# Turning h by VectorE as it comes about, in place of turning it again in the gate stage

## The chip, the core and the metric

The kernel runs on one core of one Trainium2 chip. Five engines, TensorE (PE), VectorE (DVE), ScalarE (ACT), GpSimd (POOL) and SyncE (SP), each take their own instructions in order and meet at semaphores. The metric is device time in microseconds; less is better. One execution is also profiled.

## The reference

One step of a layer of a streaming encoder over 2048 new frames and 32 frames of a running stream, 1024 channels, float32:

```python
hn = rmsnorm(h, g_mix)
proj = hn @ w_in                       # then two mixers: a short convolution, pooling windows
...
h = h + jnp.concatenate([yA, yB], axis=-1) @ w_out
gate = jax.nn.sigmoid(rmsnorm(h, g_ple) @ w_ple_gate)
h = h + (p @ w_ple) * gate
...
return rmsnorm(h, g_final), ...
```

The case turns on the line with `w_out`, which makes h, and the line with `w_ple_gate`, which needs h with channels on the partitions.

## The kernel before, in words

The work goes through stages in time: the projection w_in with the mixers (to about 545 us), some of the embedding p @ w_ple (to 553), **w_out's stage** (553 to 715), the rest of the embedding (715 to 755), the **gate stage** (755 to 924) and a tail.

Frames come in 17 tiles: sixteen of 128 frames and a short one of 32. In both stages two tiles are taken together as a pair (loop L1327 in w_out's stage; the pair of tiles i and i+1 is called oi there). A pair is multiplied by a 1024x1024 weight with seven products in place of eight (`seven`): the frames' parts are named 11, 12, 22 and the sums S1 to S4 (`frame_parts`, L193; each made by a DVE add or subtract), the weights' parts 11, 21, 22 and the differences T1 to T4. Every part is split in a high and a low half (`split`, L76 to L78: an ACT copy, a DVE subtract), and each product is 12 matmuls of 128x512 into one of three PSUM banks, X, Y and Z. The banks are read between products by DVE: a *carry* keeps a partial result (`c_o`), an *out* adds the final one into x (L1234). Products of X follow each other, so X must have been read before the next of them starts: 11·11, S2·T2, S3·T3, 22·T4 in that order.

In w_out's stage the mixers' result y, already turned, is loaded from memory (y_d) as two tiles of 512 KB for each pair (`load_y`, L314), x is loaded for each tile (`load_rows`, L327), and when both halves of a tile of x hold h, `done_h` (L1260) sums its squares on ACT (into rs_h by GpSimd, L69 and L73) and stores the tile to h_d from SyncE's queue. In the same stage the gate's weight rows are scaled: `gs` loaded by GpSimd (L1284), scaled by ACT, stored to g_d from ACT's queue.

In the gate stage h is loaded again in two ways: as it is, for the final sum, and turned, for the products. The turning differs for the two tiles of a pair:

- `turned` (the even tile and the short one): one load of h_d, two ACT copies that bring the channels in the gate's order (`ho`), eight PE transposes into two PSUM banks (`pth`, L1396).
- `turned_here` (the odd tile): four loads of 32 partitions each in pieces of 1 KB, and a DVE transpose of 32x32 blocks in place (`hn`, L1407). The gate's weight rows are kept in memory in the matching order of channels.

Buffers: pool `ya` (5 of 128x1024: y, first x, the upper rows of w_out, then hn, e and others), `qa` (2 of 128x512: gs, then ho), `xh` (3: x and h), `st`, `ss`, `cmb` for carries, sums and splits. A buffer's next load waits until the last reader of its old content is done. A scheduler orders each engine's instructions from the program; `tc.issue_after` and `tc.keep_in_program_order` hold some of them in place. SyncE issues the loads of y, x and the stores of h one after the other, each waiting for what it needs, so a load that waits holds up all that stand behind it.

Of the kernel before, what the change touches and what calls it, by code (L numbers as in the profile page):

```python
# [15 lines left out]
P = 128  # L16
D = 1024
# [17 lines left out]
def trunk(ctx, tc, x_p, x_s, c_conv, c_pool, p_p, p_s, g_mix, w_in, conv_w, conv_b, pool_w,  # L35
# [9 lines left out]
    e_d = tc.dram_tile([T, D], F32, name="e_d")  # L45
    g_d = tc.dram_tile([D, D], F32, name="g_d")
# [283 lines left out]
    with ExitStack() as s1:  # L330
# [884 lines left out]
    with ExitStack() as s2:  # L1215
        pool = lambda name, bufs: s2.enter_context(tc.tile_pool(name=name, bufs=bufs, reuse_waits="tile"))
        w3, qa, xh, st, ss, cmb = (pool(*a) for a in (
            ("w3", 1), ("qa", 2), ("xh", 3), ("st", 4), ("ss", 3), ("cmb", 8)))
# [43 lines left out]
        def prep_h(i):  # L1262
            lo, hi = load_y(i, 2 * P) if i else first_y
            S[i], more = frame_parts(cmb, ss, f"y{i}", lo[:, :, :P], hi[:, :, :P], lo[:, :, P:], hi[:, :, P:])
            return more

        def short(name, parts, n):
            A = []
            for half, t in enumerate(parts):
                c = cmb.tile([P, KH, 2, P], F32R, tag="c", name=f"{name}_{half}")  # L1270
                c = c.rearrange("p k h n -> p k (h n)")
                split(c[:, :, :n], c[:, :, n:2 * n], t[:, :, :n])
                A.append(c)
            return A

        def scale_gate(k):
# [4 lines left out]
            ts = [qa.tile([P, NH], F32, tag="q", name=f"gs_{k}_{half}") for half in range(2)]  # L1281
# [35 lines left out]
        more = prep_h(0)  # L1317
# [9 lines left out]
        for i in range(0, NT - 1, 2):  # L1327
            with tc.issue_after(loaded[-1].ins):
                x = [load_rows(xh, "x", i + b, x_p) for b in range(2)] if i else [first_x, second_x]
            seven(f"o{i}", S.pop(i), W, *h_ops(x, P, f"o{i}", i == 0), {0: {1: rest}, 2: {3: next_gate}}.get(i, {}), True, i == 0)  # L1330
            for b in range(2):
                done_h(i + b, x[b])
            last = i + 4 == NT - 1
            if last:
                n = tiles[NT - 1][1]
                A = short("yl", load_y(NT - 1, n), n)
# [27 lines left out]
        def ring(what, i):  # L1364
# [4 lines left out]
            return ring4(ya, f"e{what}_{i}")  # L1369
# [16 lines left out]
        def turned(i):  # L1386

            r, n = tiles[i]
            t = load_rows(ya, "hn", i, h_d).rearrange("p (q k c) -> p k q c", q=4, k=KC)
            out = []  # L1390
            for half in range(2):
                pt = tbank(f"pth_{i}_{half}")
                o = qa.tile([P, KH, P], F32, tag="q", name=f"ho_{i}_{half}")
                nc.scalar.copy(o[:n].rearrange("p k (q c) -> p k q c", q=4), t[:n, half * KH:half * KH + KH])
                for k in range(KH):
                    nc.tensor.transpose(pt[:, k * P:k * P + n], o[:n, k], ident[:n, :n])  # L1396
                out.append(pt.rearrange("p (k t) -> p k t", k=KH))
            return out

        def turned_here(i):  # L1400

            r, n = tiles[i]
            t = ring4(ya, f"hn_{i}")
            for q in range(4):
                nc.sync.dma_start(t[q * 32:q * 32 + 32].rearrange("p (g c) -> p g c", g=4),
                                  h_d[r:r + P, q * 256:q * 256 + 256].rearrange("(g p) c -> p g c", p=32))
            nc.vector.transpose(t, t)  # L1407
            u = t.rearrange("p (g k t) -> p k g t", g=4, k=KC)
# [47 lines left out]
        def last_pair(i, A):  # L1456
# [6 lines left out]
            e = load_rows(ya, "e", i, e_d)  # L1463
# [65 lines left out]
        def prep_g(i):  # L1529
# [4 lines left out]
            def put(q, src, view=lambda t: t):  # L1534
                A[q] = cmb.tile([P, KH, 2, P], F32R, tag="c", name=f"g{i}_{q}")
                split(view(A[q][:, :, 0]), view(A[q][:, :, 1]), src)

            def comb(q, x, y, op, view=lambda t: t):
                t = ss.tile([P, KH, P], F32, tag="s", name=f"g{i}_f{q}")
                nc.vector.tensor_tensor(view(t), x, y, op=op)  # L1540
                return t

            lower = []

            def first():
                lower.extend(turned_here(i + 1))

            def second():
                a21, a22 = lower
                s1 = comb("S1", a21, a22, ALU.add, whole)  # L1550
                a11, a12 = turned(i)
                put("11", a11)
                s2 = comb("S2", s1, a11, ALU.subtract)
                s3 = comb("S3", whole(a11), a21, ALU.subtract, whole)
                put("12", a12)
                put("S2", s2)
                s4 = comb("S4", a12, s2, ALU.subtract)
                put("S1", s1)
                put("S3", s3)
                put("S4", s4)  # L1560
                put("22", a22, whole)
# [6 lines left out]
        A = short("gl", turned(NT - 1), n)  # L1568
# [4 lines left out]
        h, e = (load_rows(*a) for a in ((xh, "h", NT - 1, h_d), (ya, "e", NT - 1, e_d)))  # L1573
# [39 lines left out]
```

## Time and profile before

| what | value |
|---|---|
| median of 3 runs | 937.44 us (937.44, 938.89, 936.55) |
| profiled execution | 935.15 us, of which the span of instructions 933.4 us |
| mean granted TensorE clock | 0.998 |
| PE busy | 917.5 us, 98% of the span |
| DVE / ACT / POOL busy | 716.9 / 482.2 / 126.3 us |
| DMA moved | 190.05 MB, 204 GB/s in the mean |

How to read it: busy time is a mean over stages; the chain of waits says what ended last; the timelines give each instruction's start, its length, and in brackets the engine's idle time before it and what ended that. Times of a timeline count from the span's start.

### The profile page before, as it was taken

To read this page: it belongs to the slowest core of one execution; us is meant where nothing else is said; L and a number is where in the kernel's file an instruction comes from. 1 tells how busy PE (TensorE), PEld (TensorE's weight loads), DVE (VectorE), ACT (ScalarE), POOL (GpSimd) and SP (SyncE) were. 2 spreads that over 40 slices of the span, in tenths; PEclk is the share of its full clock that TensorE was granted. 3 is DMA by queue.
4 is the path that set the end of the run, shared out by engine and by line. 5 is a ranking of instruction groups with operands and counts; after the bars stand their busy time and mean duration, and the time that the engine had idled before them with its cause. 6 is when DMAs were issued, how large, how long until landed. Compare 5 with 4: busy or idle time off the path is not lost.

```text
span 933.4 us, 13100 instructions
## 1 busy us (share of the span) xinstructions
PE 917.5 (98%) x4581; PEld 827.8 (89%) x4581; DVE 716.9 (77%) x1215; ACT 482.2 (52%) x895; POOL 126.3 (14%) x244
## 2 busy tenths in 40 slices
PE   8999999899999999999999999999999999999996
PEld 7999999899999999999999987888878868888885
DVE  7997988989577868585777679665564798888985
ACT  7734564644445554443545446344334875555664
POOL 3111132211001110000000011111211001211113
PEclk9999999999999999999999999999999999999999
DMA  9357587597945547328656359766775884566563
GB/s 266 84 157 221 182 269 223 182 290 259 415 134 153 161 155 206 123 87 278 199 169 175 127 194 289 251 184 196 222 228 174 321 270 121 206 225 233 194 208 113
DMA packets 133791, 190.05 MB, mean 204 GB/s; under 512 B 11740, under 2 KB 101084, under 8 KB 132445
## 3 DMA queue, kind: packets, MB, share of 16 engines
q1 hardware_dynamic: 117741, 138.78, 47.5%
q0 software_dynamic: 13248, 44.93, 14.8%
q10 hardware_dynamic: 2736, 5.51, 1.8%
q8 instruction: 36, 0.59, 0.3%
q14 instruction: 30, 0.25, 0.1%
HBM read 129.59 MB, written 59.58 MB: 203 GB/s over the span
## 4 chain that ended last, share of the span: by engine, by line
PE 75%; DMA 2%; ACT 2%; issue 1%; DVE 1%; POOL 0%; POOLq 0%; DVEq 0%; ACTq 0%
PE x_o L167 9%; PE x_g L167 9%; PE x_zab L577 5%; PE e L102 5%; PE z_g L167 5%; PE z_o L167 4%; PE x_ch L577 4%; PE x_zbv L577 4%; PE z_zab L577 2%; PE y_g L167 2%; PE z_ch L577 2%; PE y_o L167 2%; PE b L577 2%; PE z_zbv L577 2%; PE c L577 2%; PE v L577 2%
## 5 line engine op out<-in xcount | busy, mean ns | idle before, releaser
L77 ACT CAST y_S<-y_fS 128x512 fp32r<-128x512 f32 x32 | 19.5, 622 | 43.7 <-PE x_o L167 19.2
L102 PE MATMUL e<-wq,pps 128*128 128x512 f32 (+1 forms) x156 | 38.9, 399 | 0.2 <-ACT pps L77 0.2
L167 PE MATMUL x_g<-wg_b,g_S 128*128 128x512 f32 x128 | 35.9, 390 | 0.0
L167 PE MATMUL x_o<-wo_b,y_S 128*128 128x512 f32 x128 | 35.8, 391 | 0.0
L577 PE MATMUL x_zab<-B,w_zab_S 128*128 128x416 f32 x168 | 34.6, 353 | 1.0 <-DVE w_zab_S L78 0.7
L577 PE MATMUL z_ch<-B,w_ch_S 128*128 128x416 f32 x168 | 34.3, 352 | 0.9 <-ACT U L973 0.9
L577 PE MATMUL z_zab<-B,w_zab_S 128*128 128x416 f32 x168 | 34.1, 351 | 0.5 <-ACT U L973 0.5
L577 PE MATMUL x_zbv<-B,w_zbv_S 128*128 128x416 f32 x168 | 34.2, 352 | 0.3 <-ACT zs L973 0.3
L577 PE MATMUL z_zbv<-B,w_zbv_S 128*128 128x416 f32 x168 | 34.2, 352 | 0.0
L577 PE MATMUL x_ch<-B,w_ch_S 128*128 128x416 f32 x168 | 34.1, 351 | 0.0
L102 PEld LDWEIGHTS e<-wq,pps 128*128 128x128 f32 (+1 forms) x156 | 27.4, 182 | 6.9 <-ACT pps L77 0.5
L577 PEld LDWEIGHTS x_zab<-B,w_zab_S 128*128 128x128 f32 x168 | 31.1, 188 | 2.2 <-DVE w_zab_S L78 1.0
L577 PEld LDWEIGHTS z_ch<-B,w_ch_S 128*128 128x128 f32 x168 | 31.2, 188 | 1.6 <-ACT U L973 1.2
L577 PEld LDWEIGHTS z_zab<-B,w_zab_S 128*128 128x128 f32 x168 | 31.3, 188 | 1.1 <-ACT U L973 0.8
L577 PEld LDWEIGHTS x_zbv<-B,w_zbv_S 128*128 128x128 f32 x168 | 31.3, 188 | 1.0 <-ACT zs L973 0.6
L577 PEld LDWEIGHTS x_ch<-B,w_ch_S 128*128 128x128 f32 x168 | 31.3, 188 | 0.5 <-ACT c_s L973 0.2
L577 PEld LDWEIGHTS z_zbv<-B,w_zbv_S 128*128 128x128 f32 x168 | 31.3, 188 | 0.4
L69 POOL TENSOR_SCALAR ms_f<-ssq_f 128x1 f32<-128x1 f32 (+1 forms) x15 | 8.8, 588 | 160.7 <-ACT junk L88 160.7
L77 ACT CAST y<-y 128x512 fp32r<-128x512 f32 x24 | 14.9, 620 | 28.7 <-PE z_o L167 12.8
L1435 DVE SCALAR_TENSOR_TENSOR h<-h,rstd_f,g_bc 128x1024 f32<-128x1024 f32 (+1 forms) x15 | 19.3, 1284 | 12.7 <-POOL rstd_f L73 12.7
L412 DVE SCALAR_TENSOR_TENSOR xt<-xt,rstd_x,g_bc 128x1024 f32<-128x1024 f32 (+2 forms) x14 | 17.9, 1282 | 13.9 <-POOL rstd_x L73 12.7
L167 PEld LDWEIGHTS x_o<-wo_b,y_S 128*128 128x128 f32 x128 | 24.0, 188 | 5.1 <-ACT c_o L1239 0.3
(583 smaller groups left out, 2662.5 us busy)
## 6 DMA issues: line engine op xcount, KB each, us to landing
y<-y_d SPq DMA_DIRECT2D x16, 512.0 KB, 10.2
x<-in_x_prompt_dram SPq DMA_DIRECT2D x16, 512.0 KB, 6.2
h_d<-x SPq DMA_DIRECT2D x16, 512.0 KB, 4.2
h<-h_d SPq DMA_DIRECT2D x16, 512.0 KB, 3.7
xt<-in_x_prompt_dram SPq DMA_DIRECT2D x15, 512.0 KB, 6.8
e<-e_d SPq DMA_DIRECT2D x15, 512.0 KB, 5.8
out_dram<-h POOLq DMA_DIRECT2D x14, 512.0 KB, 3.0
p_dT<-T POOLq DMA_DIRECT2D x12, 512.0 KB, 6.2
```

Of the source, the lines that this page charges most:

```text
L69: nc.gpsimd.tensor_scalar(ms[:n], ssq[:n], scalar1=1.0 / D, scalar2=EPS, op0=ALU.mult, op1=ALU.add)
L77: ins = nc.scalar.copy(hi, src)
L102: nc.tensor.matmul(ps[:n], pps[:, a, k, :n], wp[k][b][:, cs], start=k + q == 0, stop=k == 1 and q == 2)
L167: nc.tensor.matmul(ps[:n], lhs[:, k, a, :n], w[b][:, k], start=start and k + q == 0, stop=k == KH - 1 and q == 2, skip_group_check=True)
L412: nc.vector.scalar_tensor_tensor(xt[:n], xt[:n], r[:n], g_bc[:n], op0=ALU.mult, op1=ALU.mult)
L577: nc.tensor.matmul(ps[:, :NB], lhs[:, k, x], b[:, k, y], start=start and k + q == 0, stop=stop and k == KH - 1 and q == 2, skip_group_chec ...
L1435: nc.vector.scalar_tensor_tensor(h[:n], h[:n], rf[:n], g_bc[:n], op0=ALU.mult, op1=ALU.mult)
```

## The change

Every tile of h is turned once, by DVE, in w_out's stage, as soon as it is complete, and is stored turned to a new place in memory in the gate's order of channels (`t_d`, and `t_s` for the short tile), by four GpSimd DMAs of 128 KB in pieces of 1 KB. The first tile of a pair is closed and turned before the pair's last product (`first_done` at step 6 of `seven`), the second after the first product of the next pair (`turn_second` at step 1). The gate stage then loads every turned tile with one plain load, and the ACT copies, the PE transposes and the gate's own DVE transposes are gone; the parts are split and combined from that tile rather than from PSUM.

To make room, `ya` has 3 buffers instead of 5, and a new pool `yb` has 2 (upper rows of w_out, the turned tile `ht`, an embedding output, and e in the gate stage); `qa` is one buffer of 128x1024 instead of two of 128x512, and holds gs and then the turned upper tile of every second pair. The loads of y for pair i+2 stand ahead of pair i's products in the program. The scheduler's order for PE stays the same but for the 72 transposes, the place of S3·T3 in pair o2 (now after four of the Y product's twelve matmuls instead of ahead of them), and the last pair, where it begins 22·T4 ahead of 11.

In the order of each engine, as built, this becomes: on DVE in each steady pair the first tile's transpose stands ahead of the add that closes the second tile, the second tile's behind the first carry of the next pair, and S1 of pair i+4 in pair oi as before; in o2 S1 of pair 4 stands ahead of the carry after S2·T2. On SyncE's queue the second half of y stands, from pair o6 on, behind both loads of x.

```diff
+    t_d = tc.dram_tile([SEQ // P, P, D], F32, name="t_d")
+    t_s = tc.dram_tile([P, D // 4], F32, name="t_s")
...
-                ya = ctx.enter_context(tc.tile_pool(name="ya", bufs=5, side="right"))
+                ya, yb = (ctx.enter_context(tc.tile_pool(name=n, bufs=b, side="right")) for n, b in (("ya", 3), ("yb", 2)))
                 first_y = load_y(0, 2 * P)
-                first_x = load_rows(ya, "x", 0, x_p)
-                tops = [ring4(ya, f"wo_q{i}") for i in range(2)]
+                tops = [ring4(yb, f"wo_q{i}") for i in range(2)]
                 for k in range(KH):
                     load_top(k, tops[k // 2])
+                first_x = load_rows(ya, "x", 0, x_p)
...
-            ("w3", 1), ("qa", 2), ("xh", 3), ("st", 4), ("ss", 3), ("cmb", 8)))
+            ("w3", 1), ("qa", 1), ("xh", 3), ("st", 4), ("ss", 3), ("cmb", 8)))
...
+        def turn_h(i, x):
+            r, n = tiles[i]
+            t = ring4(yb, f"ht_{i}")
+            tc.keep_in_program_order(nc.vector.transpose(t[:n], x[:n]))
+            g = n // 32
+            to = (t_d[i] if g == 4 else t_s).rearrange("(q c) (g n) -> g c q n", q=4, g=g)
+            for b in range(g):
+                nc.gpsimd.dma_start(to[b], t[b * 32:b * 32 + 32].rearrange("c (q n) -> c q n", q=4))
...
-            ts = [qa.tile([P, NH], F32, tag="q", name=f"gs_{k}_{half}") for half in range(2)]
+            t = qa.tile([P, D], F32, tag="q", name=f"gs_{k}")
+            ts = t[:, :NH], t[:, NH:]
...
                 x = [load_rows(xh, "x", i + b, x_p) for b in range(2)] if i else [first_x, second_x]
-            seven(f"o{i}", S.pop(i), W, *h_ops(x, P, f"o{i}", i == 0), {0: {1: rest}, 2: {3: next_gate}}.get(i, {}), True, i == 0)
-            for b in range(2):
-                done_h(i + b, x[b])
+                if i + 2 < NT - 1:
+                    y = load_y(i + 2, 2 * P)
+            def first_done():
+                done_h(i, x[0])
+                turn_h(i, x[0])
+
+            steps = {1: rest if i == 0 else turn_second, 3: next_gate if i == 2 else lambda: None, 6: first_done}
+            seven(f"o{i}", S.pop(i), W, *h_ops(x, P, f"o{i}", i == 0), steps, True, i == 0)
+            done_h(i + 1, x[1])
+            turn_second = partial(turn_h, i + 1, x[1])
...
-                    more = prep_h(i + 2)
+                    more = prep_h(i + 2, y)
...
                 done_h(NT - 1, x)
+                turn_h(NT - 1, x)
             next_gate()
+        turn_second()
...
-        def turned(i):
+        def turned(i, pool=ya):
             r, n = tiles[i]
-            t = load_rows(ya, "hn", i, h_d).rearrange("p (q k c) -> p k q c", q=4, k=KC)
-            out = []
-            for half in range(2):
-                pt = tbank(f"pth_{i}_{half}")
-                o = qa.tile([P, KH, P], F32, tag="q", name=f"ho_{i}_{half}")
-                nc.scalar.copy(o[:n].rearrange("p k (q c) -> p k q c", q=4), t[:n, half * KH:half * KH + KH])
-                for k in range(KH):
-                    nc.tensor.transpose(pt[:, k * P:k * P + n], o[:n, k], ident[:n, :n])
-                out.append(pt.rearrange("p (k t) -> p k t", k=KH))
-            return out
-
-        def turned_here(i):
...
-            nc.vector.transpose(t, t)
-            u = t.rearrange("p (g k t) -> p k g t", g=4, k=KC)
+            g = n // 32
+            t = pool.tile([P, D], F32, tag="t" if pool is ya else "q", name=f"hn_{i}")
+            nc.sync.dma_start(t[:, :g * 256], t_d[i] if g == 4 else t_s)
+            u = t[:, :g * 256].rearrange("p (g k t) -> p k g t", g=g, k=KC)
             return u[:, :KH], u[:, KH:]
...
             def first():
-                lower.extend(turned_here(i + 1))
+                upper.extend(turned(i, ya if i % 4 else qa))
+                lower.extend(turned(i + 1))
...
-            e = [load_rows(ya, "e", i + b, e_d) for b in range(2)]
+            e = [load_rows(yb, "e", i + b, e_d) for b in range(2)]
```

More of the change, by code (lines that the diff above doesn't have):

```diff
@@ L1 @@
 from contextlib import ExitStack
+from functools import partial
 from itertools import chain
@@ L1316, in trunk @@
         S = {}
-        more = prep_h(0)
+        more = prep_h(0, first_y)
         gate_rows = iter(range(KC))
@@ L1335, in trunk @@
                 n = tiles[NT - 1][1]
-                A = short("yl", load_y(NT - 1, n), n)
+                A = short("yl", [t[:, :, :n] for t in load_y(NT - 1, n)], n)
             if i + 2 < NT - 1:
                 with tc.issue_after(loaded[-1].ins), tc.issue_after(hold[-1].ins):
-                    more = prep_h(i + 2)
+                    more = prep_h(i + 2, y)
                 more()
@@ L1368, in ring @@
                 return cmb.tile([P, D], F32, tag="c", name=f"eout_{i}")
-            return ring4(ya, f"e{what}_{i}")
+            return ring4(yb if what == "out" else ya, f"e{what}_{i}")
         _, run = embed(rest_e, wp, ring)
@@ L1462, in last_pair @@
             nc.sync.dma_start(pt, p_p[(i + 1) * P:(i + 2) * P])
-            e = load_rows(ya, "e", i, e_d)
+            e = load_rows(yb, "e", i, e_d)
             wp = embedding_chunks("wl")
@@ L1567, in trunk @@
         n = tiles[NT - 1][1]
-        A = short("gl", turned(NT - 1), n)
+        A = short("gl", [t[:, :, 0] for t in turned(NT - 1)], n)
         for step in prep_g(0).values():
@@ L1572, in trunk @@
             run(c)
-        h, e = (load_rows(*a) for a in ((xh, "h", NT - 1, h_d), (ya, "e", NT - 1, e_d)))
+        h, e = (load_rows(*a) for a in ((xh, "h", NT - 1, h_d), (yb, "e", NT - 1, e_d)))
         plain("gl", A, W, n, *short_ops(h, e, n))
```

41 lines of the change are left out of this document (18 added, 23 removed).

## The prediction

> **What bounds the kernel now.** I read the page first: busy time, chain, and from issue to landing.
>
> ```profile
> span 933.4 us, 13100 instructions
> ...
> PE 917.5 (98%) x4581; PEld 827.8 (89%) x4581; DVE 716.9 (77%) x1215; ACT 482.2 (52%) x895; POOL 126.3 (14%) x244
> ...
> PE 75%; DMA 2%; ACT 2%; issue 1%; DVE 1%; POOL 0%; POOLq 0%; DVEq 0%; ACTq 0%
> ...
> x<-in_x_prompt_dram SPq DMA_DIRECT2D x16, 512.0 KB, 6.2
> h_d<-x SPq DMA_DIRECT2D x16, 512.0 KB, 4.2
> ...
> e<-e_d SPq DMA_DIRECT2D x15, 512.0 KB, 5.8
> ```
>
> TensorE works for 98% of the span and makes up most of the chain. So only two things count: work taken off PE, and waits that PE is made to take. Then the chain in order of time, cut to the gate stage's turning; columns are start, length, engine, tile, line, count.
>
> ```profile
> 749.25 0.61 PE pth L1396 x8
> ...
> 758.35 0.87 PE pth L1396 x8
> ...
> 896.68 0.87 PE pth L1396 x8
> ```
>
> There are nine such groups, one short one and eight of 0.87 us, all on the chain. Last, the timelines of PE, VectorE (DVE) and SyncE's queue (SPq) for one pair of w_out's stage, tiles 10 and 11, "o10"; its seven products begin at 650.11, from which I count below.
>
> ```profile
> 650.11 2.88 PE L167 MATMUL x_o<-wo_c,y 128*128 128x512 f32 x12
> 666.60 2.88 PE L167 MATMUL x_o<-wo_T,y 128*128 128x512 f32 x12
> 669.32 2.88 PE L167 MATMUL x_o<-wo_c,y 128*128 128x512 f32 x12
> ```
>
> ```profile
> 651.03 0.32 SPq L1260 DMA_DIRECT2D h_d<-x  x1
> 651.44 0.45 SPq L327 DMA_DIRECT2D x<-in_x_prompt_dram  x1
> 654.35 0.37 SPq L314 DMA_DIRECT2D y<-y_d  x1
> 655.34 0.33 SPq L327 DMA_DIRECT2D x<-in_x_prompt_dram  x1
> ```
>
> ```profile
> 653.03 0.69 DVE L1234 TENSOR_TENSOR c_o<-x_o,x 128x512 f32<-128x512 f32 x1 [2.03 <-PE x_o L167]
> 656.83 0.69 DVE L1234 TENSOR_TENSOR c_o<-x_o,x 128x512 f32<-128x512 f32 x1 [1.91 <-PE x_o L167]
> 663.99 0.69 DVE L193 TENSOR_TENSOR y_fS<-y,y 128x512 f32<-128x512 f32 x1 [3.89 <-issue]
> 665.33 0.68 DVE L1234 TENSOR_TENSOR x<-x_o,c_o 128x512 f32<-128x512 f32 x1
> 669.65 0.68 DVE L1234 TENSOR_TENSOR x<-x_o,x 128x512 f32<-128x512 f32 x1
> ```
>
> The row at 663.99 is the weak place. It is S1 of pair 14, the sum of that pair's two y tiles, the second of which SyncE issued at 654.35. DVE had stood still for 3.89 us, with no engine named. What it lacked was that tile, so I read its landing as about 663.9, 9.6 us after its issue. DVE takes its instructions in order, and behind S1 stands the read that frees PE's X bank (665.33, over at 666.01). PE needs that bank at 666.60. So S1 has 0.59 us left: it may start at +14.5 of a pair, and here started at +13.9. In this one pair the present kernel loads y as late as the changed one does in many.
>
> **The change part by part.** *Gain.* The 72 transposes leave PE: 0.61 + 8 x 0.87 = 7.6 us. With them go ScalarE's copies ahead of them, and the gate stage's eight transposes on DVE:
>
> ```profile
> L1407 DVE STREAM_TRANSPOSE hn<-hn x8: 1235/1236/1239, 756.1 to 895.2; 128x1024 f32<-128x1024 f32 x8
> ```
>
> ```profile
> 803.60:823.60 20.00, 20.00 (x94) 16.62 (x93) 16.58 (x25) 11.40 (x20) 3.42 (x6) 1.00 0.62 210
> ```
>
> The second fence is a stretch of the gate stage (after its length, busy PE, PEld, DVE, ACT and POOL; granted clock, DMA share, GB/s). DVE works 16.6 of 20.0 us, less 1.24 for the transpose, so it keeps up with a pair shorter by 0.87. The loads of turned h become one plain load each. A new matter there is that e now has two buffers of its own (yb), so a tile's load waits until the pair before has added e into h:
>
> ```profile
> 809.03 1.29 DVE L1428 TENSOR_TENSOR h<-h,e 128x512 f32<-128x512 f32 x2
> 815.06 0.68 DVE L1427 TENSOR_TENSOR e<-e,c_g 128x512 f32<-128x512 f32 x1
> ```
>
> The first of the two adds ends near 809.7; with 5.8 from issue to landing e is there at 815.5, 0.4 late for the row at 815.06. The transpose that leaves DVE there (1.24) covers this. I put it at 0; without that cover it is at most 0.4 x 7, 3 us.
>
> *The transposes moved.* DVE now turns 17 tiles in w_out's stage, two in a pair, 2 x 1.24 us. The first stands before the add that closes the pair before (like 669.65), the second behind the first carry (like 653.03). Normally DVE waits 2.03 and 1.91 us for PE around the latter, so the second transpose is hidden. The first is hidden only while S1 is on time: from S1 at 663.99 to 669.65 DVE already works without a pause.
>
> *Four stores for each tile*, 128 KB each, issued by GpSimd: 65 DMAs. An issue of GpSimd that exists costs 0.75 (its timeline); the windows and the DMA queues of pair o10 follow:
>
> ```profile
> 653.04 0.75 POOL L1284 DMA_DIRECT2D gs<-in_w_ple_gate_dram  x1 [2.24 <-DMA g_d<-gs]
> ```
>
> ```profile
> 650.10:669.30 19.20, 19.20 (x85) 15.69 (x84) 11.06 (x18) 6.42 (x11) 3.50 (x6) 1.00 0.70 201
> ```
>
> ```profile
> q1 hardware_dynamic: 1543, 2.78, 48.3%
> q0 software_dynamic: 544, 0.53, 11.4%
> ```
>
> Eight a pair are 6 us on an engine busy for 3.5 of 19.2; what is queued behind them, rs_h and the gate's gs loads, is wanted a pair later or in the gate stage. The bytes cost more. GpSimd's queue (q0) moved 0.53 MB for 11.4% of 19.2 us, 2.2 us of all 16 engines; 1.05 MB a pair are then 4.3 us, and a share of 0.70 becomes 0.92.
>
> Here a rule speaks against the change. The Trainium skill, "DMA: Bandwidth & Descriptors", section "Issuing engines are not separate DMA queues", says that DMAs started by different engines end up on the same 16 DMA engines and interleave. The two queue rows above, shares of one set of 16 engines, agree. By that rule SyncE's y loads pay for the stores; if the stores had a path of their own, the terms for them below would be 0 and the waits of PE about 5 us smaller.
>
> *The new wait.* With three buffers instead of five for y, and with loads of y moved in the order, SyncE's queue in pairs o6, o8 and o10 has the second half of y behind both loads of x. The second of those waits until the last h_d store of the pair before has landed: 651.03 + 4.2 = 655.2, as the row at 655.34 shows. So y is issued at +5.6 instead of +4.2, but what counts is what is in front of it. Before, it landed at +13.8. Now 0.52 MB of x goes first: at 201 / 0.70 = 287 GB/s that is 1.8 us. Of the stores, those of the first tile, half, are ahead: 2.1 us. The DMA engines have idle time to give, so I take 0.70 of the 3.9, 2.7, giving +16.5 against a limit of +14.5: PE waits 2.0, in three pairs 6. Bounds: y lands 6.2 after issue like the median x, at +11.8, and PE waits 0; all is ahead (1.8 + 4.3), and it waits 5.4 in each. I take the value nearest to the row at 663.99, the only y load of this form. A late S1 also makes the closing add late, hence the next h_d store and the next y: 0.5 for each of o8 and o10, 1 in all. In o4 y has one x ahead as before, so only stores count: 0.7 x 2.1 = 1.5, +15.3, a wait of 0.8 (0 to 3.6).
>
> *Pair o2* is special. S1 of pair 4 now stands there ahead of the carry that frees X for S3·T3:
>
> ```profile
> 571.80 0.33 SPq L1260 DMA_DIRECT2D h_d<-x  x1
> 569.28 0.68 DVE L193 TENSOR_TENSOR y_fS<-y,y 128x512 f32<-128x512 f32 x1
> 580.47 0.68 DVE L1234 TENSOR_TENSOR c_o<-x_o,x 128x512 f32<-128x512 f32 x1
> 581.51 2.88 PE L167 MATMUL x_o<-wo_b,y_S 128*128 128x512 f32 x12
> ```
>
> Its second y load waits for the first h_d store to land: 571.80 + 4.2 = 576.0, and some 2 us more, since y of pair 2 also comes later than 569.28; about 578. Landing after 6.2 to 9.6 us is 584.2 to 587.6; S1, a split and the carry (three of 0.68) put PE's S3·T3 at 586.2 to 589.6 instead of 581.51. In the changed order PE has four of the Y product's twelve matmuls ahead of it (0.9), so it loses 3.8 to 7.2. If the store lands early and y in 6.2, it is near 1. I take 4, the lower end.
>
> Sum: -7.6 + 4 + 0.8 + 6 + 1 = +4.2. Against the profiled execution of 935.15 that is 939.4; the median of the runs, 937.44, is 2.3 higher, and I forecast on it: 941.6, rounded to 942.
>
> **The rivals.** *y comes in time.* Were y to land about 6 us after issue everywhere, S1 would start near +12, within the limit of +14.5; only o2 would pay, 1 to 4, and the gain would stay: 937.44 - 7.6 + 2 = 932. For it: the median x load, same size, takes 6.2, and y loads are now spread more evenly. Against it: 9.6 in the row at 663.99 with less in front. It decides wherever y needs under 8.9 us from its issue (14.5 - 5.6). The Trainium skill, "DMA: Bandwidth & Descriptors", section "Anatomy of one DMA — SWDGE (gpsimd) path", has a fit of about 2.0 us plus bytes at 436 GB/s, by which 512 KB take an estimated 3.2 us and this rival would hold; no row here bears that out, 4.2, 5.8 and 6.2 being medians.
>
> *The stores in full ahead of y.* With the share at 0.92 the queues do not empty in time: PE waits 5.4 in o6, o8 and o10, 3.6 in o4, 7 in o2, 27 in all. Time 937.44 - 7.6 + 27 = 957. For it: o2 and the last pairs have more transfers still; against it: while PE waits, the queues drain.
>
> *The gate stage keeps its period*, because e in two buffers, or DVE, holds it where pth did: 7.6 is lost and the waits come on top, 942 + 7 = 949. The rows at 809.03 and 815.06 leave it little room.
>
> **How the numbers follow.** The forecast, late y with PE waiting some 12 us in sum (8 to 17, so 938 to 947), gets 0.50; y in time 0.28 (930 to 935); stores in full 0.15; the gate's period 0.07. About 0.3%, 2.8 us, is what a measurement of this kernel can tell from no change. Faster by more takes most of the rival with y in time: 0.26. Within it lie that rival's upper edge and the forecast's lower one: 0.16. Slower: 0.58. For 8 in 10 the range runs from 931, with nearly all of the early-y case, to 952, with the gate rival and the lower part of the stores' case. The forecast alone would be 938 to 947.
>
> **What would show it.** In the changed profile the chain should hold no pth, and the gate's pairs start 19.0 to 19.1 us apart instead of some 19.9. In w_out's stage the S1 rows of DVE should show an idle time that no engine ends, in o2, o4, o6, o8 and o10, and PE's wo_T product in o6 to o10 should start later than +16.5 by 2 to 3 us, wo_b in o2 by about 4. The DMA share there should be near 0.9. If S1 starts before +14.5 in every pair and PE's products follow without gaps, the early-y rival was right; if PE's gaps exceed 5 us a pair, the stores' rival; if the gate's pairs stay above 19.8, the third.

## The result and the profile after

The changed kernel took 947.71 us (median of six runs, 944.72 to 949.49), the kernel before 937.22 beside it: a ratio of 1.0112, 95% interval 1.0100 to 1.0125. It is 10.5 us slower, where the forecast had 4.6. The profiled execution of the changed kernel took 947.97, its span 946.2 against 933.4. Its page, the lines that answer to those shown of before:

```profile
span 946.2 us, 13043 instructions
...
PE 914.0 (97%) x4509; PEld 820.5 (87%) x4509; DVE 728.7 (77%) x1224; ACT 473.3 (50%) x877; POOL 161.3 (17%) x309
...
PE 61%; DMA 8%; DVE 7%; ACT 2%; issue 2%; POOL 1%; POOLq 0%; DVEq 0%; SPq 0%; ACTq 0%
```

PE is busy only 3.5 us less, not 7.6, in part since some products now run at half clock (below). Transfers have come onto the chain with 8% where they had 2%, and DVE with 7% where it had 1%. Where the 12.8 us between the two spans lie is read from PE's starts, counting one stage after the other: 1.7 up to pair o0, in stages that the change leaves alone (this part differs between executions: 22·T4 of o0 starts at 570.6 before and at 575.1 in d_more, whose program is the same up to there); 8.5 in **w_out's stage** (22·T4 of o0 to 22·T4 of the last pair: 141.85 before, 150.34 after); 0.1 from there to the embedding; 5.1 at **the gate's start** (first product of the rest of the embedding to first product of the first whole pair: 47.66 and 52.80); -5.5 from there to the last computation, where six pairs gain 0.9 each and the last one 0.1; 2.9 **behind the last computation**.

*The gate's pairs.* In the chain of the changed kernel no `pth` is left, and the same product returns every 19.04 us; before, the pairs stood 19.94 apart:

```profile
833.67 5.44 PE x_g L170 x24
852.71 5.44 PE x_g L170 x24
871.75 5.44 PE x_g L170 x24
890.79 5.44 PE x_g L170 x24
```

*w_out's stage.* 22·T4 started late in o2 by 3.96 us, in o4 by 0.67, in o6 by 0.05, in o8 by 1.92 and in o10 by 1.80 (each counted from the same product of the pair before it). The timelines of PE, DVE and SyncE's queue in o8 (first row) and o10:

```profile
655.62 2.97 PE L170 MATMUL x_o<-wo_T,y 128*128 128x512 f32 x12 [1.78 <-DVE x L1237]
676.62 3.00 PE L170 MATMUL x_o<-wo_T,y 128*128 128x512 f32 x12 [1.50 <-DVE x L1237]
```

```profile
674.46 0.69 DVE L196 TENSOR_TENSOR y_fS<-y,y 128x512 f32<-128x512 f32 x1 [3.34 <-DMA y<-y_d]
675.19 0.69 DVE L196 TENSOR_TENSOR y_fS<-y_fS,y 128x512 f32<-128x512 f32 x1
675.80 0.68 DVE L1237 TENSOR_TENSOR x<-x_o,c_o 128x512 f32<-128x512 f32 x1
```

```profile
660.96 0.32 SPq L1263 DMA_DIRECT2D h_d<-x  x1
661.40 5.35 SPq L330 DMA_DIRECT2D x<-in_x_prompt_dram  x2
666.85 1.15 SPq L317 DMA_DIRECT2D y<-y_d  x1
```

Read from below: two loads of x are issued, the second at the end of its 5.35 us; then y. DVE stands 3.34 us until y has come, makes S1, and the read that frees bank X (675.80) ends only at 676.48. PE starts behind it. This is the forecast's late y. The DMA share of this pair, 0.70 before, is 0.85; the forecast had 0.92.

*The gate's start.* First the chain, then two rows of before, then PE, then a table of stretches (length, busy PE, PEld, DVE, ACT, POOL, granted clock, DMA share, GB/s):

```profile
730.30 10.49 DMA wg_r<-g_d
740.82 0.62 ACT wg_c L80
```

All eight such loads before, with their median from issue to landing in the last column, and before's product that answers to the last row of the fence behind it, which came without a wait:

```profile
wg_r<-g_d SPq DMA_DIRECT2D x8, 512.0 KB, 5.5
```

```profile
761.84 1.07 PE L270 MATMUL x_gl<-wg_c,gl 128*64 128x512 f32 x4
```

```profile
742.71 0.44 PE L133 MATMUL ptp<-ident,ep 128*128 128x128 f32 x2 [1.27 <-DVE pps L81]
...
775.74 1.97 PE L273 MATMUL x_gl<-wg_c,gl 128*64 128x512 f32 x4 [2.76 <-DVE c_gl L1451]
```

```profile
773.00:775.70 2.70, 0.00 (x0) 0.00 (x0) 2.67 (x6) 1.62 (x4) 0.00 (x0) 0.98 0.56 181
775.70:777.00 1.30, 1.26 (x3) 0.73 (x4) 1.30 (x3) 0.44 (x1) 0.00 (x0) 0.50 0.94 334
```

A load of the gate's weight rows takes 10.49 us; the same load took 6.0 before (issued at 719.98, landed at 725.97). ACT waits with the split for it, PE waits for ACT by way of DVE, and from then on DVE is behind: from 742.0 to 775.7 it works 30.9 of 33.7 us and waits 1.7 for one more load of `wg_r`. For its c_gl PE stands 2.76 us. The products after that run at a granted clock of 0.50.

*Behind the last computation.* The chain ends with ACT's last scaling, and then no engine computes:

```profile
939.06 0.72 ACT hg L1512
```

```profile
940.00:946.00 6.00, 0.00 (x0) 0.00 (x0) 0.00 (x0) 0.00 (x0) 0.00 (x0) 0.50 0.23 87
```

From 939.78 to the span's end are 6.4 us; before they were 3.5 (933.4 less 929.86). What lies there is GpSimd's last long instruction, a DRAIN, which the trace holds with 2.82 us before and 6.99 after. Before, the last store of the result landed after this drain was over (at 932.4; the drain ended at 931.3), so only a longer drain shows in the span: with 3.72 us (e_raw1) the end still takes 3.5.

### The profile page after: what moved, and what is told of

Its sections match the earlier page's. It is cut to its first block, busy times and chain, and to the rows that moved or that the text cites. A ratio compares the mean times of both kernels' runs of the same rounds, so it can differ in the third digit from the quotient of the medians.

```text
span 946.2 us, 13043 instructions
## 1 busy us (share of the span) xinstructions
PE 914.0 (97%) x4509; PEld 820.5 (87%) x4509; DVE 728.7 (77%) x1224; ACT 473.3 (50%) x877; POOL 161.3 (17%) x309
## 4 chain that ended last, share of the span: by engine, by line
PE 61%; DMA 8%; DVE 7%; ACT 2%; issue 2%; POOL 1%; POOLq 0%; DVEq 0%; SPq 0%; ACTq 0%
PE x_g L170 8%; PE x_o L170 6%; PE x_zab L580 5%; PE z_g L170 4%; PE x_ch L580 4%; PE x_zbv L580 4%; DMA wg_r<-g_d 3%; DMA y<-y_d 3%; PE z_zab L580 2%; PE z_ch L580 2%; PE z_o L170 2%; PE y_g L170 2%; PE z_zbv L580 2%; PE v L580 2%; PE zb L580 2%
## 5 line engine op out<-in xcount | busy, mean ns | idle before, releaser
L80 ACT CAST y_S<-y_fS 128x512 fp32r<-128x512 f32 x32 | 19.3, 620 | 41.3 <-DVE y_fS L196 14.3
L1273 POOL DMA_DIRECT2D t_d<-ht x64 | 36.2, 570 | 2.9 <-DVE ht L1269 2.2
L80 ACT CAST g_S<-g_fS 128x512 fp32r<-128x512 f32 x32 | 19.7, 623 | 27.4 <-PE z_g L170 11.4
L72 POOL TENSOR_SCALAR ms_f<-ssq_f 128x1 f32<-128x1 f32 (+1 forms) x15 | 6.2, 416 | 146.4 <-ACT junk L91 146.2
L170 PEld LDWEIGHTS x_o<-wo_b,y_S 128*128 128x128 f32 x128 | 23.9, 188 | 6.4 <-DVE c_o L1237 1.4
```

Of the source, the lines that this page charges most:

```text
L72: nc.gpsimd.tensor_scalar(ms[:n], ssq[:n], scalar1=1.0 / D, scalar2=EPS, op0=ALU.mult, op1=ALU.add)
L80: ins = nc.scalar.copy(hi, src)
L170: nc.tensor.matmul(ps[:n], lhs[:, k, a, :n], w[b][:, k], start=start and k + q == 0, stop=k == KH - 1 and q == 2, skip_group_check=True)
L1273: nc.gpsimd.dma_start(to[b], t[b * 32:b * 32 + 32].rearrange("c (q n) -> c q n", q=4))
```

## The experiments

The measures of all runs. Ratios are against the kernel before in the same runs, with their interval; the next columns are the two stages as counted above and the distance of the gate's pairs without the last, in us, then the DMAs that GpSimd issues and its last drain.

| kernel | median | ratio (95%) | w_out | gate's start | pairs | DMAs | drain |
|---|---|---|---|---|---|---|---|
| before | 937.2 | | 141.9 | 47.7 | 19.94 | 98 | 2.82 |
| changed | 947.7 | 1.0112 (1.0100-1.0125) | 150.3 | 52.8 | 19.04 | 163 | 6.99 |
| e_nostore | 935.1 | 0.9973 (0.9960-0.9985) | 147.3 | 46.9 | 19.04 | 103 | 2.99 |
| e_noturn | 933.8 | 0.9972 (0.9951-0.9992) | 145.4 | 46.6 | 19.04 | 103 | 2.99 |
| e_raw1 | 938.5 | 1.0005 (0.9994-1.0016) | 146.5 | 50.2 | 19.04 | 115 | 3.72 |
| e_raw4 | 943.6 | 1.0053 (1.0034-1.0072) | 147.9 | 49.4 | 19.04 | 163 | 5.52 |
| e_q | 971.8 | 1.0360 (1.0315-1.0404) | 174.1 | 56.0 | 19.04 | 166 | 4.46 |
| e_actq | 960.2 | 1.0238 (1.0221-1.0255) | 162.2 | 56.5 | 19.0-19.5 | 98 | 2.82 |
| e_last | 939.7 | 1.0027 (1.0015-1.0039) | 148.1 | 45.9 | 19.04 | 154 | 6.26 |
| e_o2 | 942.7 | 1.0067 (1.0050-1.0083) | 145.2 | 51.9 | 19.04 | 163 | 6.99 |
| d_more | 943.2 | 1.0054 (1.0037-1.0072) | 142.7 | 47.7 | 19.94 | 163 | 8.13 |
| e_qa1 | 937.7 | 1.0006 (0.9995-1.0017) | 142.9 | 47.6 | 19.94 | 98 | 2.82 |
| e_ya3 | 950.6 | 1.0136 (1.0121-1.0151) | 150.7 | 47.6 | 18.3-23.9 | 98 | 2.82 |
| g_both | 942.1 | 1.0045 (1.0031-1.0059) | 141.9 | 45.9 | 19.2-27.5 | 98 | 2.82 |
| e_one | 953.9 | 1.0183 (1.0161-1.0205) | 147.1 | 46.2 | 19.5-25.4 | 115 | 3.72 |
| v_all1 | 942.6 | 1.0066 (1.0051-1.0081) | 144.5 | 46.7 | 19.4-20.1 | 115 | 3.72 |
| h_half | 954.4 | 1.0175 (1.0160-1.0190) | 145.4 | 45.9 | 19.0-30.7 | 107 | 3.31 |
| v_half1 | 945.0 | 1.0094 (1.0079-1.0109) | 144.0 | 45.9 | 19.9-21.9 | 107 | 3.31 |
| v_half4 | 937.1 | 1.0015 (0.9994-1.0036) | 144.0 | 45.9 | 18.7-20.9 | 131 | 4.62 |
| h_half4o2 | 936.6 | 0.9990 (0.9979-1.0000) | 145.4 | 45.9 | 19.0-20.5 | 131 | 4.62 |

### The stores or the rest?

**e_nostore**

```diff
-            for b in range(g):
+            for b in range(g if i in (0, NT - 1) else 0):
...
-            nc.sync.dma_start(t[:, :g * 256], t_d[i] if g == 4 else t_s)
+            nc.sync.dma_start(t[:, :g * 256], t_d[0] if g == 4 else t_s)
```

> The changed kernel without 60 of its 64 full stores of turned tiles: only tile 0's four stores and the short tile's are kept, and the gate stage loads tile 0's in place of each (so its values are not h's). VectorE's transposes, the buffers, and the order on TensorE, VectorE and SyncE stay word for word. If the stores are what costs (their bytes on the DMA engines, their place on GpSimd's queue, and a longer last drain of GpSimd), pairs o8 and o10 lose their 1.8 to 2.0 us, the gate's weights come in time, the drain is back at 2.8 us, and the time is 937 to 940. If the smaller buffers and the order of the loads are what costs, w_out's stage stays some 8 us longer than before, only the drain's 3 us go, and the time is 944 to 946.

Measured: 935.1, below both expected ranges. By the two ratios the stores cost 13 us, more than the whole loss. w_out's stage keeps 5.5 us of loss, all of it in o2; o8, o10 and the gate's start lose nothing, and the end 0.2.

**e_noturn**

```diff
         def turn_h(i, x):
+            if i not in (0, NT - 1):
+                return
...
```

(The dots stand for the two lines of e_nostore.)

> As the run without the stores, and also without VectorE's transposes of those tiles in w_out's stage (VectorE has 15 instructions of 1.24 us fewer). If the transposes lie in VectorE's idle time, the same time as the run without the stores, within 1 us. If they hold up the carries and closing adds, 2 to 4 us less. What then still stands above 930 is the price of the buffers and of the order of loads.

Measured: 933.8, within the intervals the same as with the transposes. DVE's turning is as good as hidden, as forecast. In the two profiles o2 loses 1.9 less here, but o2 differs by as much between kernels of the same order (3.7 to 5.4 in e_raw4, e_last, the changed kernel, e_raw1 and e_nostore). Of the 7.6 us gained only some 3 are left even so: 3.5 go in w_out's stage (o2) and 0.8 in the last pair.

### Buffers alone

**e_qa1**: the kernel before, `qa` one buffer of 128x1024.

> The kernel before, with one change: qa is one buffer of 128x1024 for both halves of a gate weight row (and for both halves of ho) instead of two of 128x512. If the serial loading of the gate's rows through one buffer is what made the gate's weights late in the changed kernel, its last g_d stores come 5 to 10 us later and the start of the gate stage 3 to 5 us, 940 to 942. If it was the stores ahead of them on GpSimd's queue or the later end of w_out's stage, no change: 936.5 to 938.

Measured: 937.7, no effect.

**e_ya3**: the kernel before with three buffers in `ya` and two in `yb`, nothing turned.

> The kernel before with the changed kernel's buffers (three in ya, two in yb) and nothing turned or stored. If the buffers make the loss of pair o2, as the changed kernel without the stores suggests, that pair loses 3.5 to 5.5 us and the time is 941 to 943. If the loss in o2 comes from the earlier place of the y loads or from the transposes, it stays at 937 to 938.5.

Measured: 950.6, a miss of both. The loss is spread (o2 1.7, o4 1.9, o8 1.2, o12 3.5, a gate pair of 23.9). This says that two buffers fewer are not free, not what they cost in the changed kernel.

### Number, form or bytes of the stores

Three kernels with all orders of PE, DVE and SyncE as in the changed kernel, word for word.

**e_raw1**

```diff
-            for b in range(g):
-                nc.gpsimd.dma_start(to[b], t[b * 32:b * 32 + 32].rearrange("c (q n) -> c q n", q=4))
...
+                nc.gpsimd.dma_start(t_d[i], t)
...
```

> The changed kernel with one plain store of 512 KB for each of the sixteen whole tiles, rows of 4 KB, and the gate stage's plain loads kept: the rows of turned h are left in other places than the gate wants, the work and its order on PE, DVE, SyncE's queue are the changed kernel's word for word. The bytes are the same. If the number and form of GpSimd's DMAs make the loss, w_out's pairs o8 and o10 and the gate's start lose nothing, the gate's pairs stay 19.04 apart, the last drain is near 3.7, and the time is 935 to 938. If the bytes make it, it is 944 to 948.

**e_raw4**

```diff
-            for b in range(g):
-                nc.gpsimd.dma_start(to[b], t[b * 32:b * 32 + 32].rearrange("c (q n) -> c q n", q=4))
...
+                for b in range(g):
+                    nc.gpsimd.dma_start(t_d[i, b * 32:b * 32 + 32], t[b * 32:b * 32 + 32])
...
```

> As the kernel with one plain store, but in four DMAs of 32 partitions, rows of 4 KB: the number of DMAs of the changed kernel without its pieces of 1 KB (again the reordering of the rows is left out). If the number of DMAs and GpSimd's issues make the loss, it is as slow as the changed kernel, 945 to 949, with a drain of 7. If the small pieces make it, only the drain's 3 to 4 remain: 939 to 941.

**e_q**

```diff
-            for b in range(g):
-                nc.gpsimd.dma_start(to[b], t[b * 32:b * 32 + 32].rearrange("c (q n) -> c q n", q=4))
+            for q in range(4):
+                nc.gpsimd.dma_start(to[:, :, q], t[:n, q * 256:q * 256 + 256])
```

> The changed kernel with its four stores for each tile cut along the columns instead of the partitions: each takes 256 columns of all 128 partitions, in pieces of 1 KB as before. Number, bytes, pieces and the orders of all engines stay. If 32 partitions at a time are what slows the stores and what stands behind them, o8, o10 and the gate's start come back and the drain remains: 938 to 941. If number or pieces count, it stays at 945 to 949.

Measured: 938.5, 943.6 and 971.8. By the ratios, one DMA a tile costs 3.0 us over no stores, four instead of one 4.5 more, and pieces of 1 KB instead of rows of 4 KB another 5.5, each with some 1.5 to 2 on either side; the bytes are the same in all three. So they cost at most a quarter of the stores' 13 us; number and pieces cost the rest. How the rest divides between the two is less sure: added over w_out's stage, the gate's start and the end, the profiles give 2.3, 1.9 and 7.3, and 2.3 of the 4.0 by which the first two profiled executions differ lie ahead of o0, before any store. And the 2.3 of the one DMA lie at the gate's start (50.2 against 46.9); e_one below, which stores the whole tiles in the same way and orders the gate's work otherwise, has 46.2 there. The losses of o8 and o10 together go the same way, in e_nostore, e_raw1, e_raw4 and the changed kernel: 0, 0, 2.2 and 3.7. The Trainium skill, "DMA: Bandwidth & Descriptors", section "Rules for kernel authors", says to join small transfers into one large one and not to split one over halves of the partitions: the first two kernels agree, by 4.5 us in the ratios.

e_q refuted both theories on its form: cut along the columns, the stores are far worse than in blocks of 32 partitions. Its chain has y four times with 11.4 to 11.9 us, where the changed kernel's chain has 7.9 and 7.5 (o8, o10). Three of the four:

```profile
632.53 11.79 DMA y<-y_d
657.30 11.65 DMA y<-y_d
682.06 11.86 DMA y<-y_d
```

Why is not settled; the gate's pairs, which load the same tile, are undisturbed.

**e_actq**: `nc.scalar.dma_start` for the stores.

> The changed kernel with its 65 stores issued from ScalarE's queue instead of GpSimd's; the scheduler then orders some instructions of w_out's stage otherwise. The bytes and the pieces are the same. If GpSimd's queue makes the loss, the last drain is back at 2.8 to 3.0, the gate's weight rows are stored as early as before (last near 719), and the time is 938 to 942. If the bytes make it, it stays at 944 to 948 although the drain is short; the drain's part alone would be 3 to 4 of the 10.5.

Measured: 960.2. The drain is back at 2.82, as expected, but everything else is worse, a miss of both ranges: ACT takes its instructions in order, so its splits now stand behind the stores' issues and what these wait for. PE waited 8.7 us for `pps` from ACT, 8.5 of it at once, and 8.0 for carries of DVE.

### The gate's start

**e_last**

```diff
-            for b in range(g):
+            for b in range(g if i < NT - 3 else 0):
...
-            nc.sync.dma_start(t[:, :g * 256], t_d[i] if g == 4 else t_s)
+            nc.sync.dma_start(t[:, :g * 256], t_d[min(i, NT - 4)][:, :g * 256])
```

> The changed kernel without the last nine of its 65 stores (the last pair's two tiles and the short tile; the gate stage loads the turned tile 13 in their place, so its values for these tiles are left out). All other orders are word for word the changed kernel's. If the last stores beside the loads of the gate's weights make the loss at the gate's start, the first whole pair starts 47 to 48.5 us after the embedding's first product instead of 52.8, and the time is 943 to 945 (0.6 of it the shorter drain). If the gate's rows, loaded late behind GpSimd's stores, make it, this stays at 51 to 53 and the time at 946 to 948.

Measured: 939.7. Without nine of 65 stores 8 of the 10.5 us are gone, more than either range allowed. The gate's start takes 45.90, less than before by the 1.5 of its two `pth` groups and a little. That is 6.9 us less than in the changed kernel, and the end takes 0.7 less. Another 2.2 less in w_out's stage, in o4 and o8, cannot be due to the nine, which would all come later: up to there the two kernels run the same instructions, and o8 lost 0.2 us here where it lost 1.9 there. The gate's rows were hardly late in any of these kernels: counted from the embedding's first product, the last of them is stored at +3.2 before (719.22), +3.4 in the changed kernel (729.71) and +3.1 here (726.20). So it is the stores beside the loads of `wg_r`, not the lateness of the rows. The first product of the first whole pair, and that of the embedding from which I count:

```profile
723.05 0.96 PE L105 MATMUL e<-wq,pps 128*128 128x512 f32 x3 [0.24 <-ACT pps L80]
...
768.95 0.86 PE L170 MATMUL x_g<-wg_c,g 128*128 128x512 f32 x3
```

### Pair o2

**e_o2**

```diff
-                add(t[:n], ps[:n], half_of(x, at, n))
+                c = add(t[:n], ps[:n], half_of(x, at, n))
+                if at == (0, 1) and not two:
+                    hold.append(c)
```

(`hold[-1]` is what the next pair's S1 is issued behind.)

> The changed kernel with S1 of the next pair held behind the carry after S2 x T2 in DVE's order, in every pair; loads, stores and buffers stay. If S1's place ahead of that carry makes the loss in pair o2, as the forecast said, o2's 22 x T4 comes 19.3 to 20 us after that of o0 instead of 23.0, and the time is 943 to 945. If the y load that comes late holds up pair o4 anyway, o4 loses what o2 gains and the time stays at 947 to 948.

Measured: 942.7. o2 loses 2.1 instead of 4.0, so S1's place is half of its loss. The other half is y of pair 2 itself, whose second tile is issued behind two loads of x now: in both kernels PE waits for it (1.69 us changed, 1.01 here). More than expected came from the later pairs: S1 now stands later in every pair, y has that much more time, and o8 and o10 lose nothing. S1 in o10, behind the carry at 660.24, and PE's 22·T4 without a wait:

```profile
660.85 0.68 DVE L196 TENSOR_TENSOR y_fS<-y,y 128x512 f32<-128x512 f32 x1
```

```profile
670.01 1.30 PE L170 MATMUL x_o<-wo_T,y 128*128 128x512 f32 x5
```

### The end

**d_more**: the kernel before, with small DMAs added.

```diff
+            for j in range(13 if i < 10 else 0):
+                r = i // 2 * 13 + j
+                with tc.issue_after(stored.ins):
+                    nc.gpsimd.dma_start(k_d[r:r + 1], g_bc[:1, :NH])
```

(Cut: the new place `k_d` in memory, and `stored`, the store of the pair's second tile.)

> The kernel before with 65 small DMAs more on GpSimd (2 KB each to a scratch place, thirteen behind each of five pairs in the gate stage, where GpSimd has time), so 163 as in the changed kernel; all other orders are unchanged. If the last drain grows with the number of DMAs, it takes 6 to 7 us instead of 2.82 and the time is 940 to 942. If it grows with the bytes or with DMAs still under way at the end, it stays at 2.8 and the time at 937 to 938.

Measured: 943.2, 4.9 more than the kernel before beside it (938.3), and the last drain takes 8.13. From the chain's last piece (934.97 + 0.72) to the span's end at 943.2 are 7.5 us, in which nothing computes:

```profile
934.97 0.72 ACT hg L1506
```

```profile
936.00:943.20 7.20, 0.00 (x0) 0.00 (x0) 0.00 (x0) 0.00 (x0) 0.00 (x0) 0.50 0.20 73
```

The last of the added DMAs landed at 892.1, 42 us ahead of the drain. So DMAs of GpSimd that are long done lengthen it. Their number is not all: 163 DMAs drain in 5.52, 6.99 and 8.13, 166 in 4.46. What else counts stays open.

### Other ways to turn, and a better version

**g_both**: nothing stored; DVE turns both tiles in the gate, from loads in pieces of 1 KB.

> The kernel before, with VectorE turning both tiles of a pair in the gate stage after four loads in pieces of 1 KB, as it did for the odd tile, so without TensorE's transposes and ScalarE's copies, and without any change in w_out's stage. It gives the gain alone. If VectorE keeps up (16.6 of 20.0 us before, 17.8 of 19.1 then), the gate's pairs take 19.05 us and the time is 930 to 932. If VectorE or the loads through five buffers hold it, the pairs stay at 19.5 to 20 and the time is 934 to 940.

Measured: 942.1, above both ranges, mostly by the first gate pair of 27.5 us; then 19.2 to 19.6.

**e_one**: the stores of e_raw1, with the gate's loads in four DMAs of 32 partitions.

> The changed kernel with one store of 512 KB for each turned tile in place of four of 128 KB; the tile is stored as it lies and the gate stage loads it in four DMAs of 32 partitions in pieces of 1 KB. The same bytes go the same way in w_out's stage, PE, DVE and SyncE keep their order there; GpSimd issues 17 DMAs instead of 65. If the number of GpSimd's DMAs makes the loss (its queue that holds up the gate's weight rows, its last drain), the time comes back to 936 to 939, the product wg_c of the first whole pair starts within 2 us of its place without the stores (771.5), and the last drain, 2.82 us with 98 DMAs and 6.99 with 163, is near 4 with some 115. If the bytes on the shared DMA engines make it, it stays at 945 to 948.

Measured: 953.9, a miss of both. Up to the gate's first pair it does what was expected of fewer DMAs (o8 and o10 without loss, gate's start 46.2). Then the gate's pairs take up to 25.4. SyncE's queue shows why: the loads of turned h stand behind loads of h that wait for a buffer, and PE waits for them, after which the next product too runs slowly (5.01 us for 2.88):

```profile
789.27 6.60 SPq L330 DMA_DIRECT2D h<-h_d  x2
795.92 0.90 SPq L330 DMA_DIRECT2D e<-e_d  x2
796.92 7.92 SPq L1413 DMA_DIRECT2D hn<-t_d  x8
```

```profile
791.98 5.01 PE L170 MATMUL x_g<-wg_c,g 128*128 128x512 f32 x12 [4.03 <-ACT g L80]
```

**h_half**: one tile of a pair turned and stored as in e_one, the other turned in the gate.

> The changed kernel with one tile of each pair turned and stored in w_out's stage, by one DMA of 512 KB; the other tile is loaded in pieces of 1 KB and turned by DVE in the gate stage, as the kernel before does. All PE transposes stay away, half the bytes are stored, and GpSimd issues nine DMAs more than before. If the stores' number or bytes make the loss, it is nearly gone: the gate's pairs 19.0 to 19.2 apart, w_out's stage late by o2's 4 alone, 934 to 936, so faster than before by some 2. If what remains is DVE's turning itself, it is 938 to 941.

Measured: 954.4, far above both ranges; the gate's pairs are irregular as in e_one, and SyncE's queue again stands at loads of rows that wait for a buffer (34.9 us for DVE and 29.1 for stores of the result, from 785 to 870).

**v_all1** and **v_half1**: e_one and h_half with the loads of turned h ahead of those of h and e, and S1 held as in e_o2.

> The changed kernel with one plain store a tile and the gate's loads in four, as in the earlier run, with S1 held behind the carry and the loads of turned h ahead of those of h and e in the gate stage. If the queue's order was what made the gate's pairs 19.5 to 25 us long there, they are 19.0 to 19.3 now, o2 costs under 1, and the time is 932 to 935; if the loads in pieces are too slow as such, it stays above 945.

> As the version with four stores for one tile of each pair, but one plain store for each turned tile and four loads of 32 partitions in pieces of 1 KB in the gate stage. Drain near 3.3. If the order of SyncE's queue made the earlier half version slow (its h and e loads, which wait for buffers, ahead of those of turned h), the gate's pairs are now 19.0 to 19.3 apart and the time is 931 to 934; if the eight loads in pieces themselves are too slow, the gate's pairs stay at 19.7 or above and the time over 940.

Measured: 942.6 and 945.0. The order was most of it in v_all1 (gate pairs 19.4 to 20.1 for 19.5 to 25.4), but not all. That the eight loads in pieces hold the pairs at over 19.04 is what is left; it was not shown.

**v_half4** and **h_half4o2**: one tile of a pair stored in the changed form, the other turned in the gate, S1 held; v_half4 also with turned h loaded first.

> A version meant to be faster: one tile of each pair is turned in w_out's stage and stored by four GpSimd DMAs in the changed form, the other turned by DVE in the gate as in the kernel before; S1 held behind the carry; in the gate stage the loads of turned h stand ahead of those of h and e. 33 DMAs more than before on GpSimd instead of 65. If GpSimd's number of DMAs counts, drain near 4.5, o8 and o10 without loss, gate pairs 19.0 to 19.3 apart: 932 to 935. If the gate's loads in pieces of 1 KB hold up its pairs as in the half version before, 945 or more.

> The version with half the stores in the changed form and S1 held behind the carry, with the gate stage's loads left in the order in which they come (h and e between those of turned h). The earlier run with turned h first was the same as before, 937.1, with gate pairs of 18.7 to 20.9. If that order held its pairs up, they are 19.0 to 19.3 here and the time is 933 to 935.5; if the loads in pieces do, the pairs stay irregular and the time is 936 to 940.

Measured: 937.1 and 936.6. Neither can be told from the kernel before: what the gate gains, w_out's stage (2.2 and 3.5 us) and the end (0.5, the drain being 1.8 longer) take back, and some pairs of the gate stay at 19.6 to 20.9 in either order. No version beat the kernel before by more than the measurement can tell.

## Why the prediction was right or wrong

*Right: the gate.* The gain is there, 0.90 in every pair, DVE and the two buffers for e do not stand in the way; the third rival is out. The turning on DVE is hidden (e_noturn).

*Right in size: the waits in w_out's stage,* 8.5 against 11.8. o2 was put at 4 and lost 3.96, o4 0.8 and 0.67, o8 and o10 2.0 each with a feedback of 1 in all, and lost 1.92 and 1.80. Part of this nearness is luck. S1's place, the step that the forecast named in o2, is half of o2's loss (e_o2); the rest is a wait for pair 2's own y, and in kernels of the same order o2 lost 3.7 to 5.4. And o8 lost 0.2 in e_last by the same instructions: its y took 6.5 there for 7.9. o6, put at 2.0, lost 0.05: its y was issued at 624.47, 6.5 after the pair's start, and S1 began at 632.20, +14.3, just inside the limit of +14.5.

*Two errors that cancel in o10.* This is luck too. y was to be issued at +5.6 and take 10.9; it was issued at +8.4 (666.85 less 658.43) and took 7.5, so that S1 stood at +16.0 where +16.5 was said. The second x came 5.4 after the h_d store's issue, where the 4.2 of the median had been taken. And the price of the stores was worked out from their bytes, 2.1 us ahead of y. e_raw1 moves the same bytes and o8 and o10 lose nothing: the right size stood on a wrong reason. The first rival, y in time, did not hold; the fit that speaks for it in the prediction is one for DMAs that GpSimd issues, while y is issued by SyncE, and the six loads of y whose landing the trace has in this stage took 3.5 to 8.3 us, not 3.2.

*Wrong: GpSimd's stores were costed through y alone.* The step that failed is the sum -7.6 + 4 + 0.8 + 6 + 1: it has no term for the stores outside w_out's pairs. The sentence that put everything but y at nothing is "Eight a pair are 6 us on an engine busy for 3.5 of 19.2; what is queued behind them, rs_h and the gate's gs loads, is wanted a pair later or in the gate stage." What it says of the gs loads held, for the gate's rows were hardly late (e_last). But it looked at one steady pair, and not at the last one, where the same stores run beside the loads of the gate's weights, with ACT, DVE and PE waiting in a row behind these. That made 6.6 us: 5.1 lost, and the 1.5 of the two `pth` groups there not gained (e_last has both back). The end was not looked at either: 65 DMAs more on GpSimd made its last drain 4.2 longer, the span 2.9 (d_more shows it by itself). The last pair's 0.8 was missed too. There PE waited 0.5 for a carry of ACT, ahead of which stood a sum that waited for DVE, and DVE had just split the embedding's weights (921.89); this is read from the timelines and was not tried alone.

With 8.5 in place of 11.8, and 5.1 + 1.5 + 2.9 + 0.8 = 10.3 added, the forecast's own sum comes to -7.6 + 8.5 + 10.3 = 11.2, against 10.5 between the medians, and 11.1 between the spans without the 1.7 up to o0.

## What to carry to other kernels

A transfer that is added costs at the place where it runs beside one that an engine is waiting for, so follow the added DMAs through the last iteration and into the next stage, not only through a steady one. Count them as well as their bytes: here the same 8 MB cost 3 us as one DMA a tile and 13 as four in small pieces, and GpSimd pays for its DMAs once more at the program's end (d_more, 4.9 us for 65). And before work is moved off an engine that is busy 98% of the time, add up what its new place takes in waits: here the place of one sum, ahead of a carry in an in-order engine, cost 4.2 us by the ratios (changed against e_o2), over half of what nine groups of transposes gave.

## What the hardware showed that was not expected

GpSimd's last drain grew with the number of DMAs that it had issued, also of those long landed, but not by their number alone: 2.82 us for 98, 2.99 for 103, 3.31 for 107, 3.72 for 115, 4.62 for 131, 6.26 for 154, and 4.46 to 8.13 for 163 to 166.

The granted clock fell to 0.50 after PE had stood for 2.76 us (changed), and as much in e_raw1 after 2.74:

```profile
769.26 1.97 PE L273 MATMUL x_gl<-wg_c,gl 128*64 128x512 f32 x4 [2.74 <-DVE c_gl L1454]
```

The four matmuls took 1.97 where they take 1.1 at full clock. The Trainium skill, "TensorE: Matmul & The Clock Gate", section "Part 1: The HAM clock gate (the "warmup" mystery)", has the clock halved after an idle window of about 3.4 us; here less was enough. In both kernels the products ahead of the wait had weights of only 64 and 32 columns, so it is not shown that the wait alone did it. Still shorter waits went both ways: after 1.96 us of standing in e_ya3 (from 690.99) and 2.00 in e_one (from 584.75) PE was at half clock 1.3 and 1.5 us after its restart; after 2.41 in e_actq (from 585.59) and 2.44 in e_raw4 (from 770.62) it was not.

Four stores cut along the columns, each over all 128 partitions, slowed the loads beside them more than four of 32 partitions with the same bytes and pieces: y took 11.4 to 11.9 us for 7.5 and 7.9, the kernel 971.8 us for 947.7.
